# Thirty-two bytes behind every weight buffer, and the first network in chunks of 7, 7 and 8

## The chip, the cores and the metric

The kernel runs on one core of one Trainium2 chip. The metric is the device time of one execution in microseconds (us); of several executions the median is given. The engines are TensorE (PE; its weight loads are listed apart as PEld), VectorE (DVE), ScalarE (ACT), GpSimd (POOL) and SyncE (SP), which issues most DMAs.

## The reference

One inference step of a small diffusion backbone, D = 1024, in float32, over 640 tokens at once: 512 latent tokens and 128 context tokens. Two layers, each a token mixer and a channel mixer ("network"):

```python
for i in range(DEPTH):                       # DEPTH = 2
    hp = modulate(xp, norm_mix_g[i], p_sh1, p_sc1)      # rmsnorm, scale, shift
    hs = modulate(xs, norm_mix_g[i], s_sh1, s_sc1)
    if i % N_MIXERS == 0:  ...               # bidirectional state-space scan (SSD)
    else:  ...                               # differential attention, 8 heads
    xp = xp + p_g1 * op
    xs = xs + s_g1 * os_
    xp = xp + p_g2 * conv_ffn(modulate(xp, norm_ffn_g[i], p_sh2, p_sc2), *ffn_p)
    xs = xs + s_g2 * conv_ffn(modulate(xs, norm_ffn_g[i], s_sh2, s_sc2), *ffn_p)

def conv_ffn(h, up_w, conv_w, conv_b, down_w):          # FFN_HIDDEN = 2816
    u = dwconv(h @ up_w, conv_w, conv_b)                # 3 taps along the tokens
    a, v = jnp.split(u, 2, axis=-1)
    return (jax.nn.silu(a) * v) @ down_w
```

Outputs are the final-normed tokens, the scan states and the new keys and values.

## The kernel before

Activations lie transposed: 8 tiles of 128 features by 640 tokens. Float32 products are made of three products of a rounded kind: every operand is split into a high part (`hi`, rounded to the type fp32r) and a low part (`lo`, the rest), and `hi*hi + hi*lo + lo*hi` is accumulated in PSUM. So each 128 x 128 weight slice costs three pairs of matmuls: `whi` with the high input, `whi` with the low input, `wlo` with the high input. A pair covers the 640 tokens as 256 and 384 columns (`HALF["A"]`, `HALF["B"]`), each with a weight load of its own. `dense_many` (line 197) is that loop; `block` (line 674) is the same for the 320-column products of a scheme with seven block products instead of eight, which the networks use from gated tile `S0` on.

Weights stream through units (`weight_units`, line 432): a unit of up to 128 x 1024 floats is loaded into one of four `raw` buffers by a DMA of SP (`prefetch`), then `cast` (line 146) makes `whi` on ACT and `wlo` on DVE (for some units of the second network, `wlo` is finished by an accumulating DMA of POOL). The casts go to three `whi` and three `wlo` buffers in the pool `wts` ("w"), and, while a network runs, two units in five go to two more of each in that network's own pool ("x", `place`, line 153). Buffers are laid one behind another in SBUF in the order in which pools and tags are first used: constants, `wts` (`raw`, `whi`, `wlo`), `acts` (19 tiles `f`, 4 `t`, 8 `hh` and 8 `hl` with the split inputs, 1 `sq`), then the pool of the stage. In a network's pool stand `fcw` (the taps of its convolution), the x buffers, and then, among others, `mh` and `ml`, the split gated tiles, `MIDS[l]` of each.

A network (`ffn`, line 640) has 22 gated tiles p. For each, two up products (one for `a`, one for `v`), an evacuation, an `epilogue` (convolution, SiLU, product, split into `mh`, `ml`). The down product is taken in chunks of gated tiles, `SUB[l]`: after the pairs up to one beyond the chunk's end, `project_out` makes 8 output tiles `po` over the chunk's gated tiles, and `gate_add` (line 317) adds each to the residual `xr` on DVE. The last chunk goes through `project_last`, which also starts the next norm.

The order of the work is the order of emission, refined by a scheduler with priorities. Small tasks (generators) advance at each `hook`. Two matter here: `mod_rest` (line 598), the modulation vectors of layer 1 as 96 reductions on DVE at line 620 with weights `mw` loaded by SP, started before network 0 and drained after the pairs of its second chunk (line 854); and `operands` (line 688), which builds the transformed inputs `T` in the buffers that `mod_rest` leaves and must be done before gated tile 16.

Of the kernel before, what the change touches and what calls it, by code (L numbers as in the profile page):

```python
# [9 lines left out]
F32 = mybir.dt.float32  # L10
F32R = mybir.dt.float32r
# [7 lines left out]
P = 128  # L19
# [14 lines left out]
NH = 32  # L34
FH = 2816
FT = FH // P
SUB = ((0, 8), (8, 15), (15, 22)), ((0, 4), (4, 8), (8, 12), (12, 16), (16, 22))
MIDS = 9, 6
DA_SCALE = 64 ** -0.5
LAM_INIT = 0.8 - 0.6 * math.exp(-0.3 * 1)  # L40
RAW = 4
# [8 lines left out]
class Step:  # L50
# [95 lines left out]
    def cast(self, upto):  # L146
        while len(self.wcast) <= min(upto, len(self.units) - 1):
            u = len(self.wcast)
            self.prefetch(u)
            n = self.units[u][1]  # L150
            r = self.wraw[u]
            kind = self.units[u][2]
            place = self.units[u][3] or ("x" if self.px and u % 5 > 2 else "w")
            wp, t, b = (self.pw, "w", 3) if place == "w" else (self.px, "x", 2)
            hi = wp.tile([P, 1024], F32R, tag=t + "hi", name=f"whi{u}", bufs=b)
            lo = wp.tile([P, 1024], F32R, tag=t + "lo", name=f"wlo{u}", bufs=b) if u else None
            if u == 0:
                half = lambda t, j: t.rearrange("p (k j m) -> p k j m", k=KT, j=2)[:, :, j, :]
                r3 = r[:, :n].rearrange("p (k m) -> p k m", k=KT)
                self.act(half(hi, 0), r3, AF.Copy)  # L160
                self.tt(half(hi, 1), r3, half(hi, 0).bitcast(F32), ALU.subtract)
            elif isinstance(kind, tuple):
                ns, j0, ia, iv = kind
                self.prefetch(u + iv)
                ra, rv = self.wraw[u + ia], self.wraw[u + iv]
                w = ns * P
                for j in range(j0, j0 + 1024 // w):
                    x = self.slot("f", f"s{j}", bufs=NF)[:, :w]
                    a, b, op = ((rv[:, :w], rv[:, w:2 * w], ALU.add), (self.s.get(0), ra[:, :w], ALU.subtract),
                                (ra[:, :w], rv[:, :w], ALU.subtract), (ra[:, w:2 * w], self.s.get(1), ALU.subtract))[j]  # L170
                    self.tt(x, a, b, op)
                    self.s[j] = x
                    c = slice(w * (j - j0), w * (j - j0 + 1))
                    self.act(hi[:, c], x, AF.Copy)
                    self.tt(lo[:, c], x, hi[:, c].bitcast(F32), ALU.subtract)
            else:
                c = slice(kind or 0, n)
                self.act(hi[:, c], r[:, c], AF.Copy)
                if u in self.summed:
                    self.act(lo[:, c], r[:, c], AF.Copy, scale=-1.0)  # L180
                    self.nc.gpsimd.dma_start(lo[:, c], self.units[u][0][:, c], accum_op=ALU.add)
                else:
                    self.tt(lo[:, c], r[:, c], hi[:, c].bitcast(F32), ALU.subtract)
            self.wcast[u] = (hi, lo)
# [454 lines left out]

    def ffn(self, l, h, nextnorm, pool):  # L640
        nc = self.nc
        cw = pool.tile([P, 2 * FT, 4], F32, tag="fcw", name=f"fcw{l}", bufs=1)
        nc.sync.dma_start(cw, self.a["fcw"][l])
        mid = {}

# [11 lines left out]
        def epilogue(p, ua, uv):  # L657
# [5 lines left out]
            self.tt(cv, ca, cv, ALU.mult)  # L663
            hi = self.slot("mh", f"mh{p}", F32R, bufs=MIDS[l], pool=pool)
            lo = self.slot("ml", f"ml{p}", F32R, bufs=MIDS[l], pool=pool)
            self.act(hi, cv, AF.Copy)
# [179 lines left out]
        self.seven = self.add(operands(sevens), 1) if l else None  # L846
        for s, (k0, k1) in enumerate(SUB[l]):
            self.down = False
# [4 lines left out]
            if s == 1 and not l:  # L853
                self.drain(self.modtask)
                self.seven = self.add(operands(sevens), 4)
            if s == len(SUB[l]) - 1 and self.modtask:
                self.drain(self.modtask)
            if s < len(SUB[l]) - 1:
                self.project_out(mid, range(k0, k1), self.gate(l, 1))
# [572 lines left out]
    def weight_units(self):  # L1432
# [9 lines left out]
        def ffn(l):  # L1442
# [3 lines left out]
            m = ns * 4 * P // 1024  # L1446
            for k0, k1 in SUB[l]:
                while done < min(k1 + 1, FT):
# [7 lines left out]
            return out  # L1456

        u = [(*x, None, None) for x in u] + ffn(0)
        v, u = u, []
        for hd in range(8):  # L1460
# [5 lines left out]
              for i in range(0, KT - 3, per) for j in (min(i + per, KT - 3),)]  # L1466
        u += [(a["w_ao"][i], D) for i in range(KT - 3, KT)]
        return v + [(*x, None, None) for x in u] + ffn(1)

    def run(self):  # L1470
# [143 lines left out]
```

## Time and profile before

| | |
|---|---|
| median of 3 runs | 1847.83 us (1846.91 to 1849.27) |
| the profiled execution's own time | 1847.95 us |
| its span, first to last instruction | 1846.2 us |
| mean granted TensorE clock | 0.994 |
| HBM read, written | 215.29 MB, 5.96 MB |
| PE busy in the span | 1802.7 us |

Stages in the span: the first tiles and the SSD mixer up to about 582 us, network 0 to about 1026, attention to about 1402 with the first tiles of network 1, network 1 to the end. A line of the page such as `L110 PE MATMUL po<-mh,whi` names the line in the source (here the helper `mm`), the engine, the operation, and output and inputs by the program's names without their numbers. The busy time of a matmul counts its latency and overlaps with the next one, so the pace is read from starts, in the timeline; there a row with x2 stands for two consecutive instructions of one group.

### The profile page before, as it was taken

What the parts mean: (1) busy time and instruction counts of PE and PEld (TensorE: products, weight loads), DVE (VectorE), ACT (ScalarE), POOL (GpSimd) and SP (SyncE); (2) the same over time, 40 slices, a digit from 0 to 9 for tenths busy, and PEclk for the clock granted to TensorE, in tenths of its full rate; (3) what the DMA queues carried; (4) which work ended last, traced back from release to release, by engine and by line L of the source; (5) the groups of instructions that cost most, each with busy time, mean ns of one, the idle gap of its engine ahead of it and who ended that gap; (6) DMA issues with size and microseconds to landing.
All of it is one profiled execution on the core that took longest, in us unless ns stands there. A gap on an engine that the chain in (4) does not pass through costs nothing.

```text
span 1846.2 us, 33204 instructions
## 1 busy us (share of the span) xinstructions
PE 1802.7 (98%) x13070; PEld 1704.8 (92%) x13070; DVE 1490.5 (81%) x2969; ACT 1038.7 (56%) x1987; POOL 49.2 (3%) x60
## 2 busy tenths in 40 slices
PE   7999999999999999999999999999999999999997
PEld 5899999999989999999999988888899999999996
DVE  5689999999748999987585878777878877768784
ACT  3489686879326441343353556656636554746561
POOL 0000000000000000000000000000000010101110
PEclk9999999999999999999999999999999999999998
DMA  9844343445533556542122211211124445546451
GB/s 337 264 135 138 99 148 105 121 137 179 187 133 104 194 183 214 194 133 78 57 82 91 80 48 60 65 55 38 55 83 110 104 114 141 126 129 154 122 137 58
DMA packets 90051, 230.28 MB, mean 125 GB/s; under 512 B 10428, under 2 KB 17192, under 8 KB 89768
## 3 DMA queue, kind: packets, MB, share of 16 engines
q1 hardware_dynamic: 81256, 207.13, 34.8%
q0 software_dynamic: 8064, 20.52, 6.6%
q8 instruction: 102, 1.67, 0.4%
q10 hardware_dynamic: 576, 0.52, 0.1%
q14 instruction: 53, 0.43, 0.1%
HBM read 215.29 MB, written 5.96 MB: 120 GB/s over the span
## 4 chain that ended last, share of the span: by engine, by line
PE 86%; DVE 6%; ACT 3%; DMA 3%; issue 2%; SPq 0%; POOL 0%; DVEq 0%; POOLq 0%; ACTq 0%
PE up L110 27%; PE po L110 25%; PE z L110 6%; PE x L110 5%; PE st L110 5%; PE yp L110 3%; PE bc L110 3%; PE q L110 2%; PE k L110 1%; PE modrow L110 1%; PE sl L110 1%; ACT whi L101 1%; PE ov L110 1%; PE v L110 1%; ACT e L101 1%
## 5 line engine op out<-in xcount | busy, mean ns | idle before, releaser
L101 ACT ACTIVATE whi<-raw 128x1024 fp32r<-128x1024 f32 (+3 forms) x243 | 227.8, 939 | 277.3 <-PE po L110 167.4
L107 DVE TENSOR_TENSOR wlo<-raw,whi 128x1024 fp32r<-128x1024 f32 (+3 forms) x207 | 227.0, 1097 | 43.0 <-ACT whi L101 37.5
L104 DVE SCALAR_TENSOR_TENSOR xr<-po,mod,xr 128x256 f32<-128x256 f32 (+2 forms) x279 | 107.8, 432 | 108.9 <-PE po L110 108.8
L110 PE MATMUL po<-mh,whi 128*128 128x256 f32 (+1 forms) x704 | 166.9, 310 | 0.0
L110 PE MATMUL po<-ml,whi 128*128 128x256 f32 (+1 forms) x704 | 166.6, 309 | 0.0
L110 PE MATMUL po<-mh,wlo 128*128 128x256 f32 (+1 forms) x704 | 166.3, 309 | 0.0
L110 PE MATMUL up<-h01l,whi 128*128 128x256 f32 (+1 forms) x596 | 146.2, 308 | 0.0
L110 PE MATMUL up<-h01h,whi 128*128 128x256 f32 (+1 forms) x596 | 146.1, 310 | 0.1
L110 PE MATMUL up<-h01h,wlo 128*128 128x256 f32 (+1 forms) x596 | 145.6, 308 | 0.0
L110 PEld LDWEIGHTS po<-mh,whi 128*128 128x128 f32 x704 | 128.0, 188 | 0.7 <-ACT mh L101 0.5
L110 PEld LDWEIGHTS po<-ml,whi 128*128 128x128 f32 x704 | 128.2, 188 | 0.2 <-DVE ml L107 0.2
L110 PEld LDWEIGHTS po<-mh,wlo 128*128 128x128 f32 x704 | 128.2, 188 | 0.0
L110 PEld LDWEIGHTS up<-h01h,whi 128*128 128x128 f32 x596 | 108.9, 188 | 1.5 <-ACT uraw L101 1.1
L110 PEld LDWEIGHTS up<-h01l,whi 128*128 128x128 f32 x596 | 109.1, 188 | 0.0
L110 PEld LDWEIGHTS up<-h01h,wlo 128*128 128x128 f32 x596 | 109.0, 188 | 0.0
L110 PE MATMUL up<-h11h,whi 128*128 128x320 f32 (+1 forms) x368 | 107.3, 309 | 0.0
L110 PE MATMUL up<-h11l,whi 128*128 128x320 f32 (+1 forms) x368 | 107.2, 309 | 0.0
L110 PE MATMUL up<-h11h,wlo 128*128 128x320 f32 (+1 forms) x368 | 107.1, 309 | 0.0
L104 DVE SCALAR_TENSOR_TENSOR cv<-uraw,fcw,cv 128x511 f32<-128x511 f32 (+1 forms) x176 | 85.3, 545 | 14.8 <-ACT cv L101 14.8
L104 DVE SCALAR_TENSOR_TENSOR ca<-uraw,fcw,ca 128x127 f32<-128x127 f32 (+1 forms) x176 | 86.7, 545 | 8.8 <-ACT ca L101 7.5
L101 ACT ACTIVATE mh<-cv 128x640 fp32r<-128x640 f32 x44 | 32.5, 738 | 88.8 <-DVE cv L107 88.8
L101 ACT ACTIVATE whi<-s 128x512 fp32r<-128x512 f32 (+1 forms) x96 | 52.8, 571 | 52.2 <-DVE s L107 22.7
(531 smaller groups left out, 5074.4 us busy)
## 6 DMA issues: line engine op xcount, KB each, us to landing
raw<-in_w_up SPq DMA_DIRECT2D x88, 512.0 KB, 3.4
mw<-in_modT SPq DMA_DIRECT2D x48, 512.0 KB, 3.8
raw<-in_w_in SPq DMA_DIRECT2D x40, 512.0 KB, 5.5
rb<-rowd SPq DMA_DIRECT2D x40, 512.0 KB, 5.4
raw<-in_w_qkv SPq DMA_DIRECT2D x24, 512.0 KB, 3.3
mr<-in_mod SPq DMA_DIRECT2D x44, 256.0 KB, 5.2
wlo<-in_w_up POOLq DMA_DIRECT2D x17, 512.0 KB, 5.2
mp<-in_modp SPq DMA_DIRECT2D x32, 256.0 KB, 5.4
```

The lines of the kernel that those rows point to most:

```text
L101: return self.nc.scalar.activation(out, in_, func, **k)
L104: return self.nc.vector.scalar_tensor_tensor(out, in0, s, in1, op0, op1)
L107: return self.nc.vector.tensor_tensor(out, a, b, op)
L110: return self.nc.tensor.matmul(out, lhsT, rhs, start=start, stop=stop, skip_group_check=more)
```

## The change

`whi` and `wlo` tiles are allocated with 1,032 floats instead of 1,024, of which the first 1,024 are used; `fcw` of layer 1 gets 8 floats behind its 176. So everything that lies behind them in SBUF moves by multiples of 32 bytes. The first network's chunks become 7, 7 and 8 gated tiles instead of 8, 7 and 7, with 8 `mh` and `ml` buffers instead of 9. No instruction gets another shape, apart from the lengths of the weight units of the down product, which follow the chunks.

```diff
-SUB = ((0, 8), (8, 15), (15, 22)), ((0, 4), (4, 8), (8, 12), (12, 16), (16, 22))
-MIDS = 9, 6
+SUB = ((0, 7), (7, 14), (14, 22)), ((0, 4), (4, 8), (8, 12), (12, 16), (16, 22))
+MIDS = 8, 6
...
-            hi = wp.tile([P, 1024], F32R, tag=t + "hi", name=f"whi{u}", bufs=b)
-            lo = wp.tile([P, 1024], F32R, tag=t + "lo", name=f"wlo{u}", bufs=b) if u else None
+            hi = wp.tile([P, 1032], F32R, tag=t + "hi", name=f"whi{u}", bufs=b)[:, :1024]
+            lo = wp.tile([P, 1032], F32R, tag=t + "lo", name=f"wlo{u}", bufs=b)[:, :1024] if u else None
...
-        cw = pool.tile([P, 2 * FT, 4], F32, tag="fcw", name=f"fcw{l}", bufs=1)
+        cw = pool.tile([P, 2 * FT * 4 + 8 * l], F32, tag="fcw", name=f"fcw{l}", bufs=1)
+        cw = cw[:, :2 * FT * 4].rearrange("p (f t) -> p f t", t=4)
```

## The prediction

> **What bounds the kernel now.** I read the page first (busy shares, chain), then the busy time by stage, then the chain in order of time inside one chunk of the first network, and last the timeline of TensorE (PE) alone at single tiles.
>
> ```profile
> span 1846.2 us, 33204 instructions
> PE 1802.7 (98%) x13070; PEld 1704.8 (92%) x13070; DVE 1490.5 (81%) x2969; ACT 1038.7 (56%) x1987; POOL 49.2 (3%) x60
> PE 86%; DVE 6%; ACT 3%; DMA 3%; issue 2%; SPq 0%; POOL 0%; DVEq 0%; POOLq 0%; ACTq 0%
> ...
> 582.75:688.36 105.61, 105.61 (x722) 105.61 (x722) 105.44 (x181) 54.03 (x68) 0.00 (x0) 1.00 0.55 180
> 688.36:744.66 56.30, 56.30 (x386) 56.30 (x386) 55.92 (x100) 10.63 (x12) 0.00 (x0) 1.00 0.66 211
> 843.30:893.10 49.80, 49.80 (x338) 49.80 (x338) 30.30 (x60) 12.70 (x20) 0.00 (x0) 1.00 0.20 64
> 1025.80:1312.00 286.20, 274.37 (x1931) 241.76 (x1931) 227.57 (x472) 177.20 (x372) 0.00 (x0) 0.99 0.18 59
> 1402.00:1846.20 444.20, 428.60 (x2952) 427.18 (x2950) 329.18 (x655) 251.33 (x417) 49.05 (x56) 0.98 0.50 120
> ```
>
> The stage rows give the window, its length, then busy time of PE, weight loads, VectorE (DVE), ScalarE (ACT) and POOL, the granted clock, and the DMA share. PE carries 86% of the chain. In the first network (the first three stage rows) it is busy for the whole window at a granted clock of 1.00: nobody keeps it waiting, so only the pace of the matmuls themselves, or their number, can move the end there. Only attention (1025.80 to 1312) leaves PE idle, 286.20 - 274.37 = 11.8 us. A change of padding adds or removes no matmul, so the question is the pace.
>
> The pace is in the chain of one chunk and in the timeline of PE. The rows below are the chain from 688 to 893 us, then the first and last of three consecutive pairs in four weight tiles:
>
> ```profile
> 688.36 56.30 PE po L110 x384
> 744.66 98.63 PE up L110 x672
> 843.30 49.80 PE po L110 x336
> ...
> 600.20 0.46 PE L110 MATMUL up<-h01h,whi 128*128 128x256 f32 x2
> 601.08 0.45 PE L110 MATMUL up<-h01h,whi 128*128 128x256 f32 x2
> ...
> 699.88 0.46 PE L110 MATMUL po<-mh,whi 128*128 128x256 f32 x2
> 700.78 0.46 PE L110 MATMUL po<-mh,whi 128*128 128x256 f32 x2
> ...
> 722.10 0.46 PE L110 MATMUL po<-mh,whi 128*128 128x256 f32 x2
> 722.98 0.46 PE L110 MATMUL po<-mh,whi 128*128 128x256 f32 x2
> ...
> 736.19 0.45 PE L110 MATMUL po<-ml,whi 128*128 128x256 f32 x2
> 737.05 0.45 PE L110 MATMUL po<-ml,whi 128*128 128x256 f32 x2
> ...
> 873.72 0.46 PE L110 MATMUL po<-ml,whi 128*128 128x256 f32 x2
> 874.62 0.46 PE L110 MATMUL po<-ml,whi 128*128 128x256 f32 x2
> ```
>
> A row with x2 is one pair: 256 and 384 columns under one weight slice (line 205 to 208). Between the two rows of each tile lie three pairs. So a pair takes 0.88/3 = 293 ns at 600 and 722 us, 0.90/3 = 300 ns at 700 and 874 us, and 0.86/3 = 287 ns at 736 us. Same instruction, same shape, same full clock, no wait: three cadences, 7 ns (2.3%) apart. That is what this change can touch.
>
> Which tile has which? The source says where operands lie. Weight, activation and x buffers have 4,096 or 2,560 bytes, multiples of 128, so all of the pools `wts` and `acts` share one remainder; call it 0. The only odd length ahead of the network's own pool is `fcw` with 704 bytes = 5.5 x 128, so what lies behind it there (`xhi`, `xlo`, `mh`, `ml`, `T`) is at 64. In a chunk of eight down tiles the buffers come as w, w, w, x, x, w, w, w (line 153). Then: input and weight both at 0 (600 us), 293; both at 64 (722 us, the fifth tile of the chunk, at x), 293; `mh` at 64 against a weight at 0 (second tile, 700 us) 300, and in the seventh tile (736 us) 287. So a difference of 64 bytes makes two cadences, and which one a tile falls into depends on what ran before. The chunk of 7 rows shows the same from its sum: 49.80/336 = 148.2 ns a matmul, against 56.30/384 = 146.6 in the chunk of 8 and 98.63/672 = 146.8 in the up tiles between.
>
> **The change part by part.**
>
> *Number of matmuls.* The down products run 8 tiles x (8+7+7) gated tiles before and 8 x (7+7+8) after: 22 each, the same 1,056 matmuls. PE pays nothing.
>
> *Chunk order.* Chunk 0 ends one pair of up tiles earlier, and the second drain of the modulation task (line 854) comes after pair 14 instead of 15, one pair (98.63/7 = 14.1 us) and an eighth of chunk 0 (56.30/8 = 7.0 us) sooner. The task is 96 DVE reductions:
>
> ```profile
> L620 DVE CUSTOM_DVE_ANT_0 mw<-mw,cbc 128x1024 f32<-128x1024 f32 x48 | 58.6, 1221 | 0.8
> L620 DVE CUSTOM_DVE_ANT_0 junk<-mw,cbc 128x1024 bf16<-128x1024 f32 x48 | 58.5, 1218 | 0.6 <-DMA mw<-in_modT 0.6
> L620 DVE CUSTOM_DVE_ANT_0 junk<-mw,cbc x48: 1210/1218/1226, 595.8 to 814.1; 128x1024 bf16<-128x1024 f32 x48
> ```
>
> It is done at 814 us, 843.3 - 814 = 29 us before the chunk that follows it; with 21 us less, 8 us are left. If that cover were gone, the eight `xr` additions of that chunk would queue behind reductions of 1.2 us each, and PE, with three PSUM tiles, would wait from the third tile on: an estimate of 5 us at worst. I take 0. Behind the drain, the transformed operands (`operands`, line 688) get one more ordinary pair before pair 16 needs them; they gain room and PE was not waiting, so 0. Their DMAs and the weights' keep count and order per tile on the SP queue; only their interleaving moves.
>
> *Eight `mh`/`ml` buffers instead of nine.* Alive at once are a chunk and one pair ahead: 8+1 before, 7+1 after, then the last 8. The next gated tile writes a freed buffer only after its own up products, which stand behind the chunk on PE anyway. Cost 0; without that cover, at most a tile, 7 us, per boundary.
>
> *Padding.* Each of the six w buffers and four x buffers is 32 bytes longer, and `fcw` of the second network too. Relative to the first weight buffer, modulo 128: `whi` at 0, 32, 64; `wlo` at 96, 0, 32; all of `acts` at 64 (6 x 32 = 192). Behind `fcw` of network 0 `xhi` at 0 and 32, `xlo` at 64 and 96, `mh`/`ml`/`T` at 0. Network 1: `xhi` 32, 64, `xlo` 96, 0, the rest at 32. So nearly every product changes its difference, and 4 to 5 in 10 get one of 32 or 96, which no weight product of this trace has. Inside a tile `whi` and `wlo` now often differ, so the difference changes every few matmuls.
>
> What a step of cadence costs: the weight products are 3 x (704+596+368+234+256+224) in their largest groups,
>
> ```profile
> L110 PE MATMUL po<-mh,whi 128*128 128x256 f32 (+1 forms) x704 | 166.9, 310 | 0.0
> L110 PE MATMUL up<-h01h,whi 128*128 128x256 f32 (+1 forms) x596 | 146.1, 310 | 0.1
> L110 PE MATMUL up<-h11h,whi 128*128 128x320 f32 (+1 forms) x368 | 107.3, 309 | 0.0
> L110 PE MATMUL up<-Th,whi 128*128 128x320 f32 x234 | 72.8, 311 | 1.8 <-ACT uraw L101 1.8
> L110 PE MATMUL z<-h00h,whi 128*128 128x256 f32 (+1 forms) x256 | 62.4, 323 | 0.0
> L110 PE MATMUL x<-h00h,whi 128*128 128x256 f32 x224 | 56.7, 332 | 0.1
> ```
>
> and, from the loops, 3 x (128 bc + 336 q, k, v + 256 y + 128 o + 144 first tiles): together 3 x 3,374 = 10,122, some 5,000 pairs. All of them 7 ns slower or faster is 5,000 x 0.0067 = 34 us; half of them, 17 us. That is the price from both sides, below nothing too: the trace has both cadences for one and the same pair of addresses.
>
> Which value? Where the difference was 64 the two cadences occur about equally (three tiles at 300 and three at 287 in the chunk of 8), mean 293.5; elsewhere it is 293. So for a mix of differences I take the 293 of the rows at 600 and 722 us: 0 us. The sum is 0 + 0 + 0 + 0: a span of 1846.2 and, with the 1.75 us around it, the profiled execution's 1847.95, which stands 0.1 above the median of 1847.83. Forecast **1848 us**.
>
> [...]
>
> **The rivals.**
>
> *Slower: the new differences hold the 300 ns cadence.* One mechanism: with a weight and its input 32 bytes, half of the known 64, out of step, the two reads get in each other's way for 7 ns more per pair than when both have one remainder. It decides as soon as over a tenth of the products (3.7 us) fall in. At half of them +17 us, 1865; at all of them +34, 1882. For it: of two known kinds of difference, the equal one never gave less than 293; and the only products in the trace with a difference of 32 or 96, attention's `ov` on a value tile behind short buffers, are no quicker:
>
> ```profile
> 1130.74 0.40 PE L110 MATMUL ov<-wTl,vh 128*128 128x512 f32 x1
> 1130.97 0.39 PE L110 MATMUL ov<-wTh,vl 128*128 128x512 f32 x1
> 1131.20 0.28 PE L110 MATMUL k<-h10l,whi 128*128 128x256 f32 x1
> ```
>
> 0.46 us for 2 x 512 columns is 0.449 ns a column; a pair at 287 has 0.448 and one at 293 has 0.458, though a matmul of 512 columns spreads what each matmul costs at its ends over more of them. Against it: another width, another neighbour.
>
> *Faster: the mix breaks the lock.* If a changing difference lets matmuls follow at the 287 cadence, half of them give -17 us, 1831, all of them -34, 1814. For it: the row at 736 us shows that nothing forbids it. Against it: DVE is busy 105.44 of 105.61 us and 55.92 of 56.30 us in the windows from 582.75, so there PE cannot gain until the reductions above move.
>
> *It doesn't do what it says.* If remainders are not the cause, and the cadence only remembers what ran before, the result is the forecast's, within 2 us.
>
> **How the numbers follow.** Forecast (no net change of pace, remainders harmless included) 0.40, own range 1840 to 1856; slower 0.34; faster 0.26. A measurement here tells about 0.2%, 3.7 us, from no change; of the forecast's 0.40 some 0.14 lies inside that, 0.12 below, 0.14 above. So faster 0.38, same 0.14, slower 0.48. Both signs hold most of the chance, so the range reaches into both rivals, past their half-way prices: 1824 to 1880.
>
> **What would show it.** Right: the windows of the first network keep PE busy throughout, the up pairs stay near 293 ns, and 384 matmuls of the last chunk take near 56.3 us. Pairs of 300 or more at 287 in a third of the tiles decide for a rival; a chain that leaves PE inside the first network (DVE `xr` behind L620) would show the chunk change to cost. Wrong altogether: cadences above 300 or below 287, which no row here has.

## The result, and the profile after

The changed kernel takes 1852.05 us (median of 18 executions, 1849.84 to 1855.34), the kernel before 1848.65 us (18 executions, 1845.31 to 1852.73). The ratio is 1.0017, 95% interval 1.001 to 1.0025: slower by 0.17%, or 3.4 us. The profiled execution has 1850.44 us, on the low side of its median, so single stages are compared below rather than spans.

From the page after, the span and the busy times:

```profile
span 1848.7 us, 33207 instructions
PE 1799.1 (97%) x13070; PEld 1700.8 (92%) x13070; DVE 1488.9 (81%) x2969; ACT 1038.2 (56%) x1987; POOL 49.2 (3%) x60
```

PE has the same 13,070 matmuls and is busy 3.6 us less than before (1802.7), while the span is 2.5 us longer. So the matmuls are no slower on the whole; PE stands still somewhere. The chain in order of time inside the first network (start, length, what) says where:

```profile
580.33 91.41 PE up L110 x624
671.74 49.06 PE po L110 x336
720.80 98.48 PE up L110 x672
819.28 49.11 PE po L110 x336
868.39 14.10 PE up L110 x96
882.51 0.70 ACT uraw L101
883.22 0.37 ACT T L101
...
889.32 5.70 PE up L110 x26
```

Up to 882.49 us PE works without a pause, and a little faster than before: the five pieces are 302.16 us for 2,064 matmuls, 146.4 ns each, against 310.34 us for 2,112 in the kernel before (105.61 + 56.30 + 98.63 + 49.80), 146.9 ns. The gain is 0.55 ns x 2,112 = 1.2 us. Then, at the end of gated tile 15, the chain leaves PE, for ACT and DVE. The timeline of PE shows three late starts in the first seven-product tile, 16 (in brackets the idle time by the modelled ends, and what ended it):

```profile
883.05 0.31 PE L110 MATMUL up<-h01h,wlo 128*128 128x320 f32 x1
885.10 0.41 PE L110 MATMUL up<-Th,whi 128*128 128x320 f32 x1 [1.74 <-ACT whi L101]
...
886.22 0.31 PE L110 MATMUL up<-h01h,wlo 128*128 128x320 f32 x1
887.88 0.41 PE L110 MATMUL up<-Th,wlo 128*128 128x320 f32 x1 [1.34 <-DVE wlo L107]
...
888.42 0.31 PE L110 MATMUL up<-T,wlo 128*128 128x320 f32 x1
889.32 0.64 PE L110 MATMUL up<-h01h,whi 128*128 128x320 f32 x1 [0.59 <-ACT uraw L101]
...
892.42 0.42 PE L110 MATMUL up<-T,wlo 128*128 128x320 f32 x1
892.68 0.31 PE L110 MATMUL up<-h01h,whi 128*128 128x320 f32 x1
```

From start to start that is 2.05, 1.66 and 0.90 us in the place of 0.147 each: 4.2 us. The twelve matmuls from 889.32 to 892.68 then take 3.36 us instead of 12 x 0.147 = 1.76: 1.6 us more. The stage rows (window, length, then busy time of PE, weight loads, DVE, ACT, POOL, the granted clock, DMA share, GB/s) give the reason, a clock at half for 3.4 us:

```profile
889.25:892.66 3.41, 3.34 (x12) 3.34 (x13) 2.19 (x5) 0.76 (x3) 0.00 (x0) 0.50 0.39 121
892.66:896.00 3.34, 3.34 (x23) 3.24 (x23) 0.98 (x2) 0.00 (x0) 0.00 (x0) 1.00 0.50 193
```

Together 5.8 us. Why are `whi` and `wlo` late? The timelines of ACT and then DVE after show what they queue behind; the last fence is ACT in the kernel before, at the same place of the work:

```profile
882.51 0.70 ACT L101 ACTIVATE uraw<-up 128x640 f32<-128x640 f32 x1 [1.92 <-PE up L110]
883.12 0.46 ACT L101 ACTIVATE T<-t 128x320 fp32r<-128x320 f32 x1
883.47 0.91 ACT L101 ACTIVATE cv<-uraw,fcw 128x640 f32<-128x640 f32 x1
884.28 0.46 ACT L101 ACTIVATE T<-t 128x320 fp32r<-128x320 f32 x1
884.64 0.40 ACT L101 ACTIVATE whi<-s 128x256 fp32r<-128x256 f32 x1
```

```profile
884.02 0.42 DVE L107 TENSOR_TENSOR s<-raw 128x256 f32<-128x256 f32 x1
884.42 1.93 DVE L104 SCALAR_TENSOR_TENSOR cv<-uraw,fcw,cv 128x511 f32<-128x511 f32 x4
...
887.40 0.42 DVE L107 TENSOR_TENSOR wlo<-s,whi 128x256 fp32r<-128x256 f32 x1
```

```profile
874.22 1.34 ACT L101 ACTIVATE whi<-s 128x256 fp32r<-128x256 f32 x4 [5.24 <-PE po L110]
```

Before, tile 16 came straight after a chunk of down tiles. A chunk asks nothing of ACT but casts (ACT is busy 12.70 of the 49.80 us of this one), so all four `whi<-s` (the summed weights of tile 16) were made at 874.22, 19 us before tile 16 began at 892.94. Now the ordinary tile 15 stands between the chunk and tile 16. The casts of the summed weights are emitted with tile 16 (`pair7`), behind the evacuation `uraw` of tile 15, and ACT takes them in that order, one right after the other in the rows. That evacuation can begin only when tile 15's last matmul is through (PE's piece of the chain ends at 882.49 us, `uraw` starts at 882.51). `finish_operands` (the two `T<-t`) stands in the same queue. On DVE it is the same: the sum `s` is made at 884.02, and `wlo`, the second late operand, comes at 887.40 behind the convolution steps `cv` of tile 15, which start at 884.42. The code looks one weight unit ahead, which covers the first six matmuls of tile 16 (882.32 to 883.05), no more.

The 5.8 us less the 1.2 are 4.6; the medians differ by 3.4, with an interval from 1.8 to 4.6. One execution need not add up to the medians. In this one the first network starts 2.4 us earlier than in the kernel before (580.33 against 582.75), whose granted clock was 0.50 from 23.76 to 27.17 us, where the changed kernel's was 1.00. And there is a second loss, in the second network. PE's waits from 1405 to 1480 us (waiting line, releaser, us in total, times, longest) are, in the changed kernel,

```profile
PE up L110 <- ACT uraw L101: 2.5, 1, 2.5
PE up L110 <- DVE wlo L107: 0.6, 1, 0.6
```

and in the kernel before 1.8 us for `uraw` alone: 1.3 us more. What makes this wait longer was not tried.

### The profile page after: what moved, and what is told of

Same layout as the page of the kernel before. It is cut to its first block, busy times and chain, and to the rows that moved or that the text cites. A ratio compares the mean times of both kernels' runs of the same rounds, so it can differ in the third digit from the quotient of the medians.

```text
span 1848.7 us, 33207 instructions
## 1 busy us (share of the span) xinstructions
PE 1799.1 (97%) x13070; PEld 1700.8 (92%) x13070; DVE 1488.9 (81%) x2969; ACT 1038.2 (56%) x1987; POOL 49.2 (3%) x60
## 4 chain that ended last, share of the span: by engine, by line
PE 87%; DVE 6%; ACT 4%; issue 2%; DMA 2%; SPq 0%; POOL 0%; DVEq 0%; POOLq 0%; ACTq 0%
PE up L110 27%; PE po L110 24%; PE z L110 6%; PE x L110 5%; PE st L110 5%; PE bc L110 3%; PE yp L110 3%; PE q L110 2%; PE v L110 2%; PE k L110 1%; PE sl L110 1%; PE modrow L110 1%; ACT whi L101 1%; PE in L110 1%; ACT e L101 1%
## 5 line engine op out<-in xcount | busy, mean ns | idle before, releaser
L110 PE MATMUL po<-mh,whi 128*128 128x256 f32 (+1 forms) x704 | 167.6, 309 | 0.3 <-ACT mh L101 0.2
L110 PE MATMUL po<-ml,whi 128*128 128x256 f32 (+1 forms) x704 | 167.1, 309 | 0.0
L110 PE MATMUL po<-mh,wlo 128*128 128x256 f32 (+1 forms) x704 | 166.5, 308 | 0.0
L110 PE MATMUL up<-h01h,whi 128*128 128x256 f32 (+1 forms) x596 | 147.1, 311 | 0.8 <-ACT uraw L101 0.6
L110 PE MATMUL up<-h01l,whi 128*128 128x256 f32 (+1 forms) x596 | 146.6, 309 | 0.0
L110 PE MATMUL up<-h01h,wlo 128*128 128x256 f32 (+1 forms) x596 | 145.9, 309 | 0.0
L110 PEld LDWEIGHTS po<-mh,whi 128*128 128x128 f32 x704 | 127.8, 188 | 1.2 <-ACT mh L101 0.8
L110 PEld LDWEIGHTS po<-mh,wlo 128*128 128x128 f32 x704 | 128.2, 188 | 0.0
L110 PEld LDWEIGHTS po<-ml,whi 128*128 128x128 f32 x704 | 128.0, 188 | 0.0
L110 PEld LDWEIGHTS up<-h01h,whi 128*128 128x128 f32 x596 | 109.1, 189 | 2.3 <-ACT uraw L101 1.3
L110 PEld LDWEIGHTS up<-h01h,wlo 128*128 128x128 f32 x596 | 109.4, 189 | 0.0
L110 PEld LDWEIGHTS up<-h01l,whi 128*128 128x128 f32 x596 | 109.3, 188 | 0.0
L110 PE MATMUL up<-h11h,wlo 128*128 128x320 f32 (+1 forms) x368 | 107.2, 309 | 0.6 <-DVE wlo L107 0.6
L110 PE MATMUL up<-h11l,whi 128*128 128x320 f32 (+1 forms) x368 | 107.1, 309 | 0.0
L110 PE MATMUL up<-h11h,whi 128*128 128x320 f32 (+1 forms) x368 | 107.1, 309 | 0.0
```

What stands on the lines that cost most here:

```text
L110: return self.nc.tensor.matmul(out, lhsT, rhs, start=start, stop=stop, skip_group_check=more)
```

## The experiments

Two theories on the 3.4 us: A, the switch from ordinary to seven-product tiles, exposed by the chunk order, costs about 6 us, and the rest of the change gives some back; B, the padding slows the matmuls and the chunks cost nothing.

**Chunks alone.** `SUB` and `MIDS` as in the change, weight buffers and `fcw` as in the kernel before.

> Chunks of 7, 7 and 8 with eight mh/ml buffers, without any padding. Theory A (the loss is at the switch from ordinary to seven-product tiles: an ordinary pair now stands between the second chunk and tile 16, and the casts for tile 16 queue behind its evacuations): TensorE starts come late three times at tile 16, 4.2 us together, the matmuls after it run some 2.4 us slow, so about 6.6 us over the kernel before, 1855 us, ratio 1.0036; and slower than the padded kernel by what its padding gains, about 3 us. Theory B (the padding costs, the chunks nothing): as the kernel before, 1848.6 us, ratio 1.000, no late start at tile 16.

Measured 1854.79 us, ratio 1.0033 (1.002 to 1.0046): +5.6 us by the medians. Two of the three late starts are there, as long as in the changed kernel; PE's timeline:

```profile
887.49 0.41 PE L110 MATMUL up<-Th,whi 128*128 128x320 f32 x1 [1.74 <-ACT whi L101]
890.27 0.64 PE L110 MATMUL up<-Th,wlo 128*128 128x320 f32 x1 [1.35 <-DVE wlo L107]
```

The third is down to 0.48 us from start to start (891.23 to 891.71). In its place the clock stands at half for twice as long as in the changed kernel:

```profile
889.75:896.57 6.82, 6.29 (x22) 5.89 (x23) 4.57 (x11) 2.60 (x6) 0.00 (x0) 0.50 0.39 124
```

In the changed kernel the 3.41 us at half clock lost 1.6 us (twelve matmuls in 3.36 us instead of 1.76); at that rate the 3.4 us more here cost another 1.6 us, an estimate. Theory B falls: without any padding the loss is there, and not smaller.

**Two units ahead, with and without padding.**

```diff
             ua = copy_out(self.next_tile(h, "up"))
-            epilogue(p, ua, copy_out(self.next_tile(h, "up")))
+            if p == S0[l] - 1 and not l:
+                self.deep = 2
+            uv = copy_out(self.next_tile(h, "up"))
+            self.deep = 2 if l else 1
+            epilogue(p, ua, uv)
```

> The changed kernel with one edit: the casts run two units ahead instead of one from the second up product of tile 15 on, so that the summed weights of tile 16 are cast before the evacuation of tile 15. Theory A: the late starts at tile 16 shrink or go; if all go, 6.6 us less than the changed kernel's 1852.05, 1845.5 us, ratio 0.998 to the kernel before; if only the wait for whi goes (2 of 4.2 us), about 1849. Theory B: no change, 1852 us.

> Chunks of 7, 7 and 8 without padding, with the casts two units ahead from the second up product of tile 15 on. Switch theory: the two late starts behind whi and wlo go as they did with padding, 5.6 us less than the same kernel without the look-ahead (1854.79), 1849.2, ratio 1.000 to the kernel before. Beside the padded kernel with the same look-ahead (1848.72) it is a third price of the padding: neutral theory, within 2 us of it; if the padding saves the 2.7 us that it seemed to save in the kernel with 7, 7 and 8, 1851.4.

Measured 1848.72 us with padding, 0.9998 (0.9988 to 1.0007), and 1848.23 without, 1.0000 (0.9991 to 1.0009). Both are back at the kernel before: 3.3 and 6.6 us less than the same kernels without the look-ahead. From ACT's timeline of the padded one, and from PE's waits there between 880 and 900 us:

```profile
880.76 1.02 ACT L101 ACTIVATE whi<-s 128x256 fp32r<-128x256 f32 x3
884.70 0.70 ACT L101 ACTIVATE uraw<-up 128x640 f32<-128x640 f32 x1 [2.91 <-PE up L110]
```

```profile
PE up L110 <- ACT uraw L101: 0.6, 1, 0.6
```

The casts now stand ahead of `uraw`, the waits for `whi` and `wlo` are gone, and only the third, shortest one is left (0.6 us). The expected 1845.5 for the padded kernel did not come: its median lies 0.3 us under the 1849 named for half a cure, though the trace shows both waits gone. By that trace the cure is worth the 5.8 us less the 0.8 of the pause that stays (0.94 instead of 0.147), 5.0 us (1.6 of them the clock); the intervals of both differences, 3.3 and 6.6, hold that.

**Seven-product tiles from 15 on, with and without padding.**

```diff
-S0 = 16, 4
+S0 = 15, 4
```

> The changed kernel with the seven-product tiles from gated tile 15 on instead of 16, so that, as in the kernel before, the first of them follows a chunk directly. Tile 15 then has 90 products of 320 columns instead of 96, 6 x 0.147 = 0.9 us less work. Theory A: no late start at the first seven-product tile, 1852.05 - 6.6 - 0.9 = 1844.5 us, ratio 0.9978 to the kernel before. Theory B: only the work goes, 1851 us, ratio 1.0013.

> Chunks of 7, 7 and 8, seven-product tiles from 15 on, no padding: beside the same with padding this prices the padding without any stall at the switch. Theory A: the kernel before less 0.9 us of work, 1847.7 us, and about 3 us more than with padding. Theory B (the padding slows the matmuls by 3.4 us or more): 1847.7 us, and 3 us less than with padding.

Measured 1844.6 us with padding, 0.9974 (0.9965 to 0.9983), and 1843.76 without, 0.9971 (0.9961 to 0.9981). The first seven-product tile follows a chunk again, and PE waits for nothing there; tile 15 as a seven-product tile also takes six matmuls fewer (13,064 in all). For the unpadded kernel this is 3.9 us better than expected. A part of it is a wait in the second network, at its own first seven-product tile; PE's waits from 1405 to 1480 us in the kernel before (with chunks alone it is 1.9 us), then in the unpadded and in the padded kernel with tiles from 15:

```profile
PE up L110 <- ACT uraw L101: 1.8, 1, 1.8
```

```profile
PE up L110 <- DVE wlo L107: 0.6, 1, 0.6
PE up L110 <- ACT uraw L101: 0.4, 1, 0.4
```

```profile
PE up L110 <- DVE wlo L107: 0.5, 1, 0.5
```

In the kernel before the clock stands at half for 3.4 us behind this wait (last section), another 1.5 us: fourteen matmuls from 1453.86 to 1457.45 us take 3.59 us instead of 14 x 0.147 = 2.06. In the two kernels with tiles from 15 it is 1.00 in the mean from 1402 to 1480 us, against 0.98 in the kernel before. The rest of the 3.9 us stays open. The added weight unit of tile 15 shifts which later units go to x buffers (`u % 5`), and this may be why that wait shrinks; it was not tried by itself.

**What the padding is worth** can now be read three times, with minus without: 1852.05 - 1854.79 = -2.7 us, 1848.72 - 1848.23 = +0.5, 1844.6 - 1843.76 = +0.8. As ratios -0.0016, -0.0002 and +0.0003, each uncertain by 0.0013 to 0.0015: the last two are not to be told from 0, the first only just. And 1.6 us of that first may be the clock, which in the profiled execution of the kernel with chunks alone stands at half for longer behind tile 15 (above), and not the pace of the matmuls. The chain shows that pace, here of the kernel with chunks alone:

```profile
582.42 91.54 PE up L110 x624
673.96 48.97 PE po L110 x336
722.92 98.61 PE up L110 x672
821.53 49.26 PE po L110 x336
870.79 14.09 PE up L110 x96
```

302.47 us, 0.3 more than with padding. So of the 1.2 us that the changed kernel gained up to tile 15, padding gave 0.3; the rest came with the chunk order.

**One difference for all products.** The prediction's ground was that a weight and its input 64 bytes out of step (modulo 128) give 287 or 300 ns a pair, and 0 gives 293. From the unpadded kernel with tiles from 15 (1843.76), three layouts keep one difference, 0, 32 and 64, in nearly all weight products:

```diff
# 0
+        cw = pool.tile([P, 2 * FT * 4 + 16], F32, tag="fcw", ...)
# 32 (for 64: 16 floats in the first line, 0 for fcw, 16 in the last)
+        self.ph.tile([P, 8], F32, tag="pad", name="pad", bufs=1)     # ahead of acts
+        cw = pool.tile([P, 2 * FT * 4 + 8], F32, tag="fcw", ...)     # x buffers as w
+                padded.append(pool.tile([P, 8], F32, tag="pad", name=f"padm{l}", bufs=1))   # ahead of mh, ml
```

> From the kernel with seven-product tiles from 15 on and unpadded weight buffers: fcw is longer by 64 bytes in both networks, so that the x buffers, mh, ml and T too have the remainder of the w buffers; every weight product of the networks has a difference of 0. Neutral theory (a difference of 64 gives 287 and 300 ns a pair by what ran before, 293.5 in the mean; 0 always 293): the down tiles of both networks show 293 ns and nothing else, time within 2 us of 1843.8. Theory that a difference costs (300): down tiles that now stand at 300 save 7 ns a pair, down tiles at 287 lose nothing: up to 3 us less. Theory that remainders have no part in it: 287 and 300 are still seen in the down tiles.

> From the same kernel: the activations, the mh and ml tiles and network 1's T lie 32 bytes out of step with every weight buffer (w and x buffers at one remainder), so nearly all weight products of the kernel have the difference 32. Slower rival (such a difference holds 300 ns a pair): 5,000 pairs x 6.7 ns = 34 us more, 1878 us. Faster rival (287): 34 us less, 1810 us. Neutral theory: the mean stays at 293 ns, 1843.8 within 4 us.

> From the same kernel: activations, mh, ml and network 1's T lie 64 bytes out of step with every weight buffer, so nearly all weight products have the difference that in the kernel before only the down products at w buffers had. Neutral theory: single tiles at 287 and at 300 ns in both networks, up products too, and which of them has which hangs on what ran before; if they come evenly, 1843.8; if the up tiles all fall into one of them, up to 34 us less or more, 1810 or 1878. Theory that remainders have no part: up products stay at 293.

Measured: 0, 1844.68 us, 0.9973 (0.9964 to 0.9983); 32, 1840.13 us, 0.9952 (0.9937 to 0.9967); 64, 1844.76 us, 0.9975 (0.9966 to 0.9984). From the chains of the first network, in this order (the inserted line makes L110 into L111 in some), the first chunk of down tiles, for 32 with the up tiles behind it:

```profile
672.21 49.28 PE po L110 x336
```

```profile
671.25 49.00 PE po L111 x336
720.25 98.00 PE up L111 x672
```

```profile
674.52 49.28 PE po L111 x336
```

At 0 and at 64 the first two chunks have one pace, 49.28/336 = 146.7 ns, a pair of 293.3, and the up tiles between them too (98.56 us for 672). The mean of a chunk could hide 287 and 300 in equal parts; read from start to start, from 691 to 700 us of the first chunk, the pairs stand at 293 in both kernels (30 of them in 8.80 us at 0, 31 in 9.09 us at 64). At 32 it is 145.8 ns, 291.7 a pair, down and up alike. The neutral theory is right at 0, but fails at 64: no pair read there stands at 287 or 300. Both rivals fail at 32: neither 300 nor 287; the neutral theory's time holds there (within 4 us of 1843.8), its 293 does not.

**Difference 64 in w buffers, 0 in x buffers.** The layout for 64, but with the 16 floats behind `fcw` instead of ahead of `mh`, so that the down tiles have the remainders of the kernel before.

> As the kernel with every difference at 64, but the x buffers too are shifted by 64 bytes, so that weight units in w buffers have a difference of 64 to the activations and units in x buffers 0, in the up tiles and the down tiles of both networks. Theory of the change (one difference kept from tile to tile gives one cadence, 293 at 0 and at 64; 287 and 300 come only after a change of the difference): 287 and 300 now in the up tiles as well, in runs of two or three tiles between x tiles at 293; the time by how many of each, at most 10 us off 1844.5 either way. Theory that the position of the buffers in the kernel before, not the change, made them: all tiles at 293, 1844.5.

Measured 1844.37 us, 0.9971 (0.9963 to 0.998). Its chain:

```profile
674.34 49.31 PE po L111 x336
```

That is 293.5 ns a pair; the up tiles behind it and the second chunk have 293.3 (98.56 us for 672, 49.28 for 336), and from 691 to 700 us 30 pairs take 8.80 us, 293 each. My first theory, that a change of the difference between w and x tiles makes 287 and 300, falls. The down tiles here have the same remainders of weights and inputs as in the kernel before, in the same alternation, and not its pace. What sets the kernel before, with its 287 and 300, and the one with chunks alone, whose chunks have 291.5 and 293.2 in the mean (48.97 and 49.26 us), apart from these is that the input's remainder changes by 64 bytes between up and down tiles; in the layouts with one pace it stays. That fits, but was not tried alone, and why it acts on some tiles and not on others stays open.

**Difference 96.** As with 32, with 24 floats in all three places.

> As the kernel with every difference at 32, with 96 instead. If only the distance in memory counts, 96 is 32 the other way round and gives 291 ns a pair in the 256 + 384 products: about 1840. If the remainder itself counts: another cadence, 287 (1830) to 300 (1860).

Measured 1846.88 us, 0.9988 (0.9979 to 0.9996). The chain has 98.58 us for 672 up matmuls, 293.4 ns a pair: 96 is not 32 the other way round.

```profile
723.25 98.58 PE up L111 x672
```

**Difference 32 in the kernel before.** Chunks of 8, 7 and 7, tiles from 16, with the three insertions for 32.

> The kernel before (chunks of 8, 7 and 7, seven-product tiles from 16), with the activations, mh, ml and network 1's T 32 bytes out of step with all weight buffers and nothing else changed. If one constant difference of 32 is what gives 291 ns: 2 to 2.5 ns for each of some 3,000 pairs of 256 + 384 columns, 6 to 7 us, about 1842, ratio 0.9965. If the gain belonged to the other chunks or to the seven-product tiles from 15: 1848.7.

Measured 1845.07 us (1839.63 to 1850.84), 0.9978 (0.9965 to 0.9991): 4.5 us less than the kernel before of the same runs (1849.53). Its chain against 105.61, 56.30, 98.63 and 49.80:

```profile
580.86 105.00 PE up L111 x720
685.86 56.00 PE po L111 x384
741.86 98.00 PE up L111 x672
839.86 49.00 PE po L111 x336
```

145.8 ns for every matmul again, 2.3 us less in this part of the first network alone. The 4.5 us, with an interval from 1.7 to 6.5, are less than the 6 to 7 expected, but clear of the 1848.7 named for the other explanations. So the gain belongs to the layout with the constant difference of 32. In the layouts with a difference of 0, 32, 64 or 96 everywhere, nearly all weights have the remainder 0, so the difference is also the input's own remainder; these runs do not tell the two apart. The quickest version of all is the one with 7, 7 and 8, tiles from 15 and that difference: 1840.13 us, 0.48% under the kernel before.

## Why the prediction was right or wrong

The forecast of 1848 with no net effect was 4 us under what came, and the sum behind it was right in three terms and wrong in one. That it came so near is in part luck: a loss of 5.8 us and a gain of 1.2 in the first network stand in no term of it, and the 0 for the padding rested on a ground that was half wrong.

- *What bounds the kernel.* Right: PE's matmuls in the first network, and the loss appears in the time as stops of PE and a slower clock behind them.
- *Number of matmuls.* Right, 13,070 both times.
- *Chunk order.* This is the step that failed. The prediction said that behind the drain "the transformed operands get one more ordinary pair before pair 16 needs them; they gain room and PE was not waiting, so 0". It looked at the buffers and the time since the drain, not at what that extra pair puts into the queues of ACT and DVE ahead of the casts for tile 16 (the rows from 882.51 to 887.40 us above). The term was put at 0 and measures 5.8 us in the trace after, 4.2 of late starts and 1.6 of half clock. Four other versions take it away: two let the casts run ahead of tile 15's evacuation, and two let the first seven-product tile follow a chunk again, each with and without padding.
- *The reductions as cover.* The "8 us left" were not. The 814 us behind them are the last of the `junk` rows; the last of the `mw` rows began at 815.4 in the kernel before. And with DVE full (busy 216.27 us of the 220 from 600 to 820), that last reduction did not move earlier but ran from 819.73 to 820.95 us, 1.7 us into the chunk that begins at 819.28. Yet the price named for lost cover, up to 5 us, was not paid: that chunk took 49.11 us for 336 matmuls, PE's ordinary pace.

```profile
819.73 1.22 DVE L620 CUSTOM_DVE_ANT_0 mw<-mw,cbc 128x1024 f32<-128x1024 f32 x1
```

- *Eight `mh`/`ml` buffers.* Right, 0: no wait at either chunk's boundary in the chain.
- *Padding.* The 0 was right as far as the three pairs of runs can tell, and for the reason given (a mix of cadences; the means after are 292.0 and 292.3 ns a pair in the first two chunks, 293.1 in the up tiles between). The ground under it was half wrong: 64 bytes of difference do not make 287 or 300 by themselves, since a constant 64 gives 293.
- *The rivals.* The slower rival's mechanism, two reads in each other's way, was a guess that no run shows, and it fell: 32 gives 291.7, not 300. The remark there on 512 columns has figures in the trace before: from start to start 0.120 us for 256 columns (1398.02 to 1400.30 us), 0.173 for 384 (1401.00 to 1405.68) and 0.23 for 512 (the `ov` rows), so 0.469, 0.451 and 0.449 ns a column. The faster rival's sign was right for that difference alone, its 287 was not reached as a steady pace, and mixed remainders did not bring it. The third rival, that the cadence remembers what ran before, holds in part: equal remainders gave 293 in one kernel and 287 to 300 in another.
- *The signs named in advance.* "A chain that leaves PE inside the first network would show the chunk change to cost": it did, at 882.49 us, though through ACT's casts and not through `xr` behind L620. The last chunk's pace could not be read as named, since the scheduler mixes other work into it.

## What to carry to other kernels

When an edit moves a phase boundary, list for ACT and DVE, which in the rows from 882.51 to 887.40 us work in the order of emission, what now stands ahead of the first casts and evacuations of the next phase; a look-ahead of one unit that a quiet phase hid is exposed by a busy one (here by 4.2 us of late starts). Give the change of phase its own deeper look-ahead, or let it follow a phase that leaves those engines free. Where alignment is suspected, make the operands' difference constant and measure each value: a mix of remainders gives a mean, and hides the one that pays (here 32, at 1840.13 us, against 1844.68, 1844.76 and 1846.88 at 0, 64 and 96).

## What the runs showed of the hardware that was not expected

The clock fell behind short stops of PE, but not behind every one. Behind the three pauses of 2.05, 1.66 and 0.90 us start to start it stood at 0.50 for 3.41 us, in the kernel with chunks alone for 6.82. In the kernel before, a single pause of 2.1 us at 1451.36 us (the 1.8 us wait for `uraw` above) was followed by half clock too, 0.50 from 1453.95 to 1457.35 us, 0.83 over 10 us:

```profile
1450.00:1460.00 10.00, 8.21 (x46) 7.95 (x45) 7.17 (x14) 7.36 (x14) 1.76 (x2) 0.83 0.39 85
```

At the same place of the work the changed kernel stops for longer, 2.79 us from start to start at 1453.91 us (the 2.5 us wait), and its clock stays at 1.00:

```profile
1450.00:1460.00 10.00, 6.90 (x45) 6.38 (x44) 9.25 (x18) 7.20 (x16) 0.89 (x1) 1.00 0.20 42
```

So the length of a stop alone does not decide, and what else does stays open. With the look-ahead, the one remaining pause at tile 16, 0.94 us start to start, left the clock at 1.00.

The pace of a pair at full clock changes with where weight and input lie: 291.7 ns at a constant difference of 32 bytes modulo 128, 293.3 at 0 and 64, 293.4 at 96, and single tiles at 287 or 300 in the kernel before, whose inputs change their remainder between up and down tiles.
